# A hybrid pooling and state-space layer on one core: masks, far tiles and column constants in another order, and two pieces of the last output in halves

## The chip, the core and the metric

The kernel runs on one core of a Trainium2 chip. The core has a matrix engine (TensorE, PE in the profile, with PEld for its weight loads), VectorE (DVE), ScalarE (ACT), GpSimd (POOL), and SyncE (SP), which here only issues DMAs. Sixteen DMA engines move data between HBM and the on-chip memory SBUF. PSUM is the memory into which TensorE accumulates. Each engine works through its own instructions in the order of the program and waits at semaphores for the others.

The metric is the time of one execution in microseconds; several executions are timed, and the median is compared. One further execution is profiled.

## The reference

One step of a layer, for a new stream of 256 frames and for a running stream of 32 more (288 tokens in all, all fp32):

```python
xn = rmsnorm(x, norm_mix_pre)
proj = xn @ w_in            # u | z | xBC | dt
y_pool = pool_mixer(u)      # trailing means over 2/4/8/16 frames, then w_pool
y_ssd, h_last = ssd_mixer(z, xbc, dt)   # causal conv, exact chunked scan, SiLU gate, grouped norm
mix = concatenate([y_pool, y_ssd]) @ w_out
x = x + rmsnorm(mix, norm_mix_post)
hn = rmsnorm(x, norm_ffn_pre)
f = (silu(conv(hn @ w_up)[gate]) * conv(hn @ w_up)[value]) @ w_down
x = x + rmsnorm(f, norm_ffn_post)
...
y = (y_diag + y_off).reshape(b, s, G, J, P) + D[..., None] * xh   # in the scan: D is ssd_d, one per head
h_last = decay * h0 + states
```

Outputs are x for both streams and the new states: the pooling rows, the rows of both convolutions, and `h_last`.

## The kernel before

**Layout.** Activations lie with channels on the 128 partitions and the 288 tokens along the row, one tile for each 128 channels. The input has `KD` = 16 tiles, the scan 16 tiles of two heads each (`xs`), the FFN 88 up tiles and 44 input tiles of w_down.

**Products in fp32r.** Each fp32 operand is split into a rounded high part and the rest. ACT copies the high part (`whi`, line 152), VectorE subtracts (`wlo`, line 153), and TensorE makes three products (high by high, high by low, low by high; `mm3`, line 166). `project` does this for groups of 128 output columns: weights come from HBM in pieces (`raw`, four buffers, sent by SP, line 137), are split into `whi` and `wlo` (four buffers each), and are multiplied, in k groups such as (0, 8), (8, 8). The first project of the FFN takes k in four groups of four tiles, and four weight pieces for each group (three of two column tiles and one of one).

**What sets the order.** The framework orders instructions by a timeline of its own, except where `pin` (keep_in_program_order) fixes them among each other, and where `issue_after` puts one behind another. A DMA waits for its buffer, and SP's DMAs go out in order.

**The stages,** in order of time:

1. The start (to 47 us). The pieces `w_first` of the first 768 columns come in 11 chunks (`CHUNKS`), are split by `prepare` (lines 318 to 344) and multiplied (line 397). Beside that the squares of the input are summed for the first norm: `squares` has ACT square two tiles at a time and VectorE add them to a sum (lines 351 to 354), through one buffer, after the chunks that `SQUARES` names. Two `prs` products (line 391) add over partitions, and `rstd` is made of them (lines 394 and 395).
2. The mixer (to 290 us). 8 rounds of `xs` projects, then 8 of `z`. A round's conv is `conv_in` and `conv_out`, with a tanh on ACT. For the scan, heads go in 8 quads. `ssd_masks` (lines 645 to 658) makes a quad's decay mask on ACT (12 Relu, one Exp) and VectorE; `XS_RATE` and `Z_RATE` say in which rounds. `run_pair` multiplies the two quads that stand ready (lines 678 to 684), in the rounds of `PAIR_XS` and `PAIR_Z`. The column constants `dcol` (line 583) hold, for each partition, D for the skip connection (16 columns) and the state's last decay (32): TensorE makes them from `pick`, `sel64` and `hv` with two products (lines 575 and 576).
3. The output product w_out (to 464 us), with the new scan state between.
4. The input of the FFN (464 to 515 us). Line 1087 gives `rm`, the factor of the norm. For each of 16 tiles VectorE multiplies by `rm` (line 1119). The residual is added for tiles 0 to 7 (`NEAR`) by VectorE from SBUF (line 1121), for tiles 8 to 15, the far ones, by a DMA of POOL that adds while it writes (line 1123). Then `hn_of` makes the FFN's input: ACT the high part (line 1100) and a square (line 1108), VectorE the low part (line 1101) and the sum of squares (line 1115). The tiles are done in order 0 to 15. Meanwhile TensorE already multiplies with the tiles that are ready (first project of w_up).
5. The FFN (to 1290 us) and the tail. At the end the token-major output y_prompt is written in 8 pieces of 128 tokens by 512 columns (256 KB each): four for tokens 128 to 255, then four for tokens 0 to 127, together the last 1 MB. For these last four, `rf` is the norm's factor. Piece 0 is made by TensorE (identity times the residual, plus a diagonal matrix of `rf` times the FFN's result, lines 1385 and 1389), copied by ACT (line 1390) and sent by ACT (line 1393). Pieces 1 to 3 are made by VectorE and sent by SP (`y_out`, lines 1367 and 1368).

Of the kernel before, what the change touches and what calls it, by code (L numbers as in the profile page):

```python
# [1 line left out]

# [6 lines left out]
F32 = mybir.dt.float32  # L9
# [3 lines left out]
AX = mybir.AxisListType  # L13
# [26 lines left out]
XS_RATE = (0, 0, 1, 0, 1, 0, 0, 1)  # L40
# [11 lines left out]
    ("f_b", 2 * NF), ("hist_f", 2 * 2 * NF),  # L52
# [4 lines left out]
NEAR = 8  # L57
W_GAP = 48
# [11 lines left out]
def body(  # L70
# [190 lines left out]
    hp = side1.tile([HEADS, 3], F32, name="hp")  # L261
# [26 lines left out]
    id32 = ident[:HEADS, :HEADS]  # L288
# [67 lines left out]
    SQUARES = {4: (0,), 5: (1,), 6: (2,), 7: (3, 4), 8: (5,), 9: (6,), 10: (7,)}  # L356
# [3 lines left out]
    for i, (kb, n) in enumerate(CHUNKS):  # L360
# [26 lines left out]
        for q, (r, m, k, x) in enumerate(products):  # L387
            if i == len(CHUNKS) - 2 and q == 24:
                p_ = aux([P, NT], "prs")
                for c in (slice(0, NT), slice(NT, 2 * NT)):  # L390
                    pin(pe.matmul(p_, ones_r, sq_r[:, c], start=c.start == 0, stop=c.start > 0))
# [5 lines left out]
            pin(pe.matmul(  # L397
                first[m], w[r][:, k, m * P : (m + 1) * P], xn[kb + k][:, x, :],
                start=kb + k + r + x == 0, stop=kb + k == KD - 1 and r == 1,
            ))  # L400
# [13 lines left out]
    act.activation(g_ssd, col["ssd_norm"], AF.Copy, scale=0.5)  # L414
    start.close()
# [4 lines left out]
    sel = mp.tile([HEADS, 2], F32, name="sel")  # L420
    pick = mp.tile([HEADS, NX], F32, name="pick")
    sel64 = mp.tile([HEADS, 2, 64], F32, name="sel64")
    with tc.issue_after(last_split[1].ins):
        dve.tensor_reduce(sel, id32.rearrange("h (t r) -> h r t", r=2), axis=AX.X, op=ALU.add)
        dve.tensor_reduce(pick, id32.rearrange("h (t r) -> h t r", r=2), axis=AX.X, op=ALU.add)
        dve.tensor_copy(sel64, sel.unsqueeze(2).broadcast_to([HEADS, 2, 64]))
# [19 lines left out]

    def conv_out(i, e, out):
# [11 lines left out]
        act.activation(th, c, AF.Tanh)  # L459
# [104 lines left out]
    p_t = aux([P, 10 * HEADS + NX], "ptok")  # L564
    p_tok = p_t[:, : 9 * HEADS].rearrange("p (b h) -> p b h", b=3)
# [3 lines left out]
    hv = htile("hv", NX + HEADS)  # L569
# [5 lines left out]
    follow(pe.matmul(p_[:, :NX], sel64.rearrange("h r q -> h (r q)"), hv[:, :NX], start=True, stop=True))  # L575
    follow(pe.matmul(p_[:, NX:], ones[:HEADS, :], hv[:, NX:], start=True, stop=True))
# [5 lines left out]
    dcol = const.tile([P, NX + HEADS], F32, name="dcol")  # L582
    dve.tensor_copy(dcol, p_)
# [48 lines left out]
    def ssd_masks(q):  # L632
# [55 lines left out]
    def ssd_add(q, ys):  # L688

        for i in range(2):  # L690
            t = 2 * q + i
            for c, y in zip((slice(0, NP_), slice(NP_, NT)), ys[i]):
                o = xs[t][:, c]
                dve.scalar_tensor_tensor(o, o, dcol[:, t : t + 1], y, op0=ALU.mult, op1=ALU.add)
# [266 lines left out]

    bt_h, bt_l = (op_.tile([P, 2, 2, P], F32R, name=n) for n in ("bt_h", "bt_l"))
# [52 lines left out]
    def history(g):  # L1015

        for i in range(2):
# [5 lines left out]
            w = dcol[:, NX:][:, heads]  # L1023
# [94 lines left out]
    for s in range(KD):  # L1118
# [5 lines left out]
        while todo and todo[0] + (1 if todo[0] < NEAR else NEAR) <= s:  # L1124
# [238 lines left out]
    def y_out(q, b, rf):  # L1363
# [3 lines left out]
        pin(dve.scalar_tensor_tensor(x, f_, rf, x, op0=ALU.mult, op1=ALU.add))  # L1367
        pin(sp.dma_start(out=y_prompt[0][b * P : (b + 1) * P, 512 * q : 512 * (q + 1)], in_=x))
# [15 lines left out]
    p_y = acc_ps.tile([P, 512], F32, tag="acc", name="py_")  # L1384
    pin(pe.matmul(p_y, ident, xr[0], start=True, stop=False))
# [3 lines left out]
    pin(pe.matmul(p_y, diag, ft[0], start=False, stop=True))  # L1389
    pin(act.activation(xr[0], p_y, AF.Copy))  # L1390
    y_out(1, 0, rf[:, 0:1])
    y_out(2, 0, rf[:, 0:1])
    pin(act.dma_start(out=y_prompt[0][0:P, 0:512], in_=xr[0]))
# [10 lines left out]
def _laid_out(v, np):  # L1404
# [6 lines left out]
    def groups(a):  # L1411
# [10 lines left out]
        v["state_ffn_conv"],  # L1422
# [7 lines left out]
        "heads": np.stack([v[n][0] for n in ("ssd_dt_bias", "ssd_a_log", "ssd_d")], axis=1),  # L1430
# [32 lines left out]
```

## Time and profile before

| | |
|---|---|
| median of the runs | 1305.62 us (1305.27 to 1305.78, 3 runs) |
| profiled execution, own time | 1306.34 us |
| its span in the profile | 1304.6 us |
| busy, share of the span | PE 99%, PEld 99%, DVE 69%, ACT 51%, POOL 19% |
| granted clock of TensorE | 1.000 |
| mean DMA rate | 193 GB/s, 251.75 MB moved |

The span goes from the first to the last instruction; the own time of the execution is longer, since it takes in what lies before and behind. A row of a timeline gives the start in microseconds, the time, the engine, the line, the operation, the tiles written and read, how many were merged, and in brackets how long the engine was idle before and what ended it. A row of a group gives busy time and mean nanoseconds of one, then idle time before. A row of the waits gives total, times and longest. A row of the chain of waits gives start, duration, engine and line of the chain that ended last. A row of DMA issues gives kilobytes each and the median time from issue to landing.

### The profile page before, as it was taken

What the parts mean: (1) busy time and instruction counts of PE and PEld (TensorE: products, weight loads), DVE (VectorE), ACT (ScalarE), POOL (GpSimd) and SP (SyncE); (2) the same over time, 40 slices, a digit from 0 to 9 for tenths busy, and PEclk for the clock granted to TensorE, in tenths of its full rate; (3) what the DMA queues carried; (4) which work ended last, traced back from release to release, by engine and by line L of the source; (5) the groups of instructions that cost most, each with busy time, mean ns of one, the idle gap of its engine ahead of it and who ended that gap; (6) DMA issues with size and microseconds to landing.
All of it is one profiled execution on the core that took longest, in us unless ns stands there. A gap on an engine that the chain in (4) does not pass through costs nothing.

```text
span 1304.6 us, 25289 instructions
## 1 busy us (share of the span) xinstructions
PE 1296.9 (99%) x10043; PEld 1286.6 (99%) x10043; DVE 897.0 (69%) x1531; ACT 671.6 (51%) x1013; POOL 251.7 (19%) x399
## 2 busy tenths in 40 slices
PE   9999999999999999999999999999999999999998
PEld 9999999999999999999999999999999999999997
DVE  7999987989655588867766744336666666664454
ACT  7557676646544567554544433334444454444442
POOL 2343231222222231211211100001111111201110
PEclk9999999999999999999999999999999999999999
DMA  8668877445767478766545455455545555466663
GB/s 329 204 211 274 250 242 232 137 166 169 242 213 229 140 198 259 210 185 202 172 162 166 160 170 175 157 175 182 174 162 166 175 175 165 163 233 191 209 182 113
DMA packets 110326, 251.75 MB, mean 193 GB/s; under 512 B 64768, under 2 KB 73888, under 8 KB 87936
## 3 DMA queue, kind: packets, MB, share of 16 engines
q1 hardware_dynamic: 103856, 233.36, 55.7%
q0 software_dynamic: 5824, 16.13, 4.3%
q8 instruction: 78, 1.28, 0.4%
q10 hardware_dynamic: 528, 0.66, 0.2%
q14 instruction: 40, 0.33, 0.1%
HBM read 237.11 MB, written 13.00 MB: 192 GB/s over the span
## 4 chain that ended last, share of the span: by engine, by line
PE 96%; DMA 1%; DVE 1%; ACT 1%; issue 0%; SPq 0%; ACTq 0%
PE acc L166 91%; PE acc_x L166 1%; DMA raw<-in_w_first 1%; PE py L678 1%; PE acc L1324 0%; DVE w L334 0%; PE acc L1325 0%; DMA xg<-in_x_g 0%; PE acc_t L1347 0%; DVE sq L354 0%; PE py L680 0%; PE acc_x L397 0%; PE acc L397 0%; DVE xn L321 0%; PE pst L1036 0%
## 5 line engine op out<-in xcount | busy, mean ns | idle before, releaser
L153 DVE TENSOR_TENSOR wlo<-raw,whi 128x1024 fp32r<-128x1024 f32 (+1 forms) x396 | 472.7, 1196 | 297.1 <-ACT whi L152 296.1
L152 ACT ACTIVATE whi<-raw 128x1024 fp32r<-128x1024 f32 (+1 forms) x396 | 408.0, 1033 | 471.1 <-PE acc L166 381.3
L166 PE MATMUL acc<-hn,whi 128*128 128x288 f32 x2752 | 539.0, 294 | 0.5 <-ACT hn L1100 0.4
L166 PEld LDWEIGHTS acc<-hn,whi 128*128 128x128 f32 x2752 | 436.3, 188 | 1.5 <-ACT hn L1100 0.8
L166 PE MATMUL acc<-hn,wlo 128*128 128x288 f32 x1376 | 399.6, 291 | 0.0
L166 PEld LDWEIGHTS acc<-hn,wlo 128*128 128x128 f32 x1376 | 259.0, 188 | 0.0
L166 PE MATMUL acc<-fa,whi 128*128 128x288 f32 x1320 | 257.5, 293 | 0.0
L166 PE MATMUL acc<-xn,whi 128*128 128x288 f32 x1216 | 238.5, 294 | 0.0
L166 PEld LDWEIGHTS acc<-fa,whi 128*128 128x128 f32 x1320 | 208.9, 188 | 0.0
L166 PEld LDWEIGHTS acc<-xn,whi 128*128 128x128 f32 x1216 | 192.9, 188 | 0.6 <-issue 0.5
L166 PE MATMUL acc<-fa,wlo 128*128 128x288 f32 x660 | 192.1, 291 | 0.0
L166 PE MATMUL acc<-xn,wlo 128*128 128x288 f32 x608 | 177.4, 292 | 0.0
L166 PEld LDWEIGHTS acc<-fa,wlo 128*128 128x128 f32 x660 | 124.3, 188 | 0.0
L1150 POOL COPY fc_stage<-ebuf 128x4 f32<-128x4 f32 x88 | 26.9, 306 | 472.8 <-DVE ebuf L1149 451.4
L166 PEld LDWEIGHTS acc<-xn,wlo 128*128 128x128 f32 x608 | 114.5, 188 | 0.0
L166 PE MATMUL acc<-mixs,whi 128*128 128x288 f32 x512 | 100.2, 293 | 0.0
L1145 POOL COPY ebuf<-cols 128x2 f32<-128x2 f32 x88 | 71.7, 816 | 111.1 <-DVE fc L1156 91.8
L1156 DVE SCALAR_TENSOR_TENSOR fc<-ebuf,cols,fc 128x290 f32<-128x290 f32 x176 | 90.5, 518 | 3.5 <-ACT fc L1154 0.8
L1154 ACT ACTIVATE fc<-ebuf,cols 128x290 f32<-128x290 f32 x88 | 54.4, 623 | 72.4 <-DVE ebuf L1149 72.4
L166 PEld LDWEIGHTS acc<-mixs,whi 128*128 128x128 f32 x512 | 81.1, 188 | 0.0
L166 PE MATMUL acc<-mixs,wlo 128*128 128x288 f32 x256 | 74.6, 291 | 0.0
L166 PE MATMUL acc<-mixp,whi 128*128 128x288 f32 x256 | 50.1, 293 | 0.0
(323 smaller groups left out, 1245.3 us busy)
## 6 DMA issues: line engine op xcount, KB each, us to landing
raw<-in_w_up SPq DMA_DIRECT2D x80, 1024.0 KB, 5.1
raw<-in_w_in SPq DMA_DIRECT2D x38, 1024.0 KB, 5.3
raw<-in_w_down SPq DMA_DIRECT2D x32, 1024.0 KB, 5.0
raw<-in_w_out SPq DMA_DIRECT2D x22, 1024.0 KB, 5.2
raw<-in_w_down SPq DMA_DIRECT2D x16, 768.0 KB, 4.4
raw<-in_w_up SPq DMA_DIRECT2D x14, 512.0 KB, 4.6
gb<-g_d POOLq DMA_DIRECT2D x8, 832.0 KB, 6.4
raw<-in_w_first SPq DMA_DIRECT2D x5, 768.0 KB, 13.0
```

Source lines behind the costliest of these rows:

```text
L152: act.activation(hi, raw[:, k : k + n, :], AF.Copy)
L153: dve.tensor_tensor(lo, raw[:, k : k + n, :], hi.bitcast(F32), op=ALU.subtract)
L166: ins = pe.matmul(out, w, a[:, x, :], start=start and n == 0, stop=stop and n == 2)
L678: ins = pe.matmul(y[c, 0:256], xw[:, 0, f_], m[:, h, 0:256], start=True, stop=False)
L1145: pool.tensor_copy(e[:, 258:260], hist_f[:, :, i])
L1150: pool.tensor_copy(fc_stage[:, :, :, i], e[:, 256:324].rearrange("p (s c) -> p s c", c=34)[:, :, 0:2])
L1154: act.activation(c, e[:, 0:290], AF.Identity, bias=col["f_b"][:, i : i + 1], scale=f_w[:, 0, i : i + 1])
L1156: dve.scalar_tensor_tensor(c, e[:, r_ : r_ + 290], f_w[:, r_, i : i + 1], c, op0=ALU.mult, op1=ALU.add)
```

## The change

Several parts, all in one kernel function and its tables:

- `SQUARES`: tiles 2 and 3 are squared behind chunk 4 too, each later pair one chunk earlier, and no chunk has two pairs after that. The two `prs` products stand at the beginning of the last chunk's products instead of at product 24 of the one before.
- `XS_RATE`: quads 0, 1, 2 are masked in xs rounds 5, 6, 7 instead of 2, 4, 7. The first quad's Relu and the Exp of `ce` are put behind a tanh.
- `dcol`, and `sel`, `pick`, `sel64`, `hv` with it, are gone. D comes as 16 more columns of the constants that are loaded at the start (`skip`, repeated over partitions by the host's layout), and the last decay goes out to HBM (`e_d`) and back in to all partitions (`kept`), two small DMAs of SP.
- The turns of the far tiles: after tiles 0 to 3 the order is 8, 4, 9, 5, 10, 6, 11, 7, 12, 13, 14, 15, and `hn_of` of a near tile is called at the turn of the next near one; those of tiles 7 to 15 after all turns.
- The tail: VectorE's first of the last four pieces (piece 1) is made and sent in two halves of 256 columns. Piece 0 has two PSUM tiles of 256 columns; each half is multiplied, copied and sent by itself, the first by SP, the second by ACT.

```diff
-XS_RATE = (0, 0, 1, 0, 1, 0, 0, 1)
+XS_RATE = (0, 0, 0, 0, 0, 1, 1, 1)
...
-    SQUARES = {4: (0,), 5: (1,), 6: (2,), 7: (3, 4), 8: (5,), 9: (6,), 10: (7,)}
+    SQUARES = {4: (0, 1), 5: (2,), 6: (3,), 7: (4,), 8: (5,), 9: (6,), 10: (7,)}
...
-            if i == len(CHUNKS) - 2 and q == 24:
+            if i == len(CHUNKS) - 1 and q == 0:
...
-    dve.tensor_scalar(hv[:, 0:NX], pick, hp[:, 2:3], None, op0=ALU.mult)
-    dve.tensor_scalar(hv[:, NX:], id32, elast, None, op0=ALU.mult)
-    p_ = p_t[:, 9 * HEADS :]
-    follow(pe.matmul(p_[:, :NX], sel64.rearrange("h r q -> h (r q)"), hv[:, :NX], start=True, stop=True))
-    follow(pe.matmul(p_[:, NX:], ones[:HEADS, :], hv[:, NX:], start=True, stop=True))
+    e_d = dram.tile([HEADS, 1], F32, name="e_d")
+    sp.dma_start(out=e_d, in_=elast)
...
-            act.activation(ce, gb[:, :, 384:], AF.Exp)
+        with ExitStack() as order:
+            if not q:
+                order.enter_context(tc.issue_after(tanhs[-1].ins))
+            act.activation(ce, gb[:, :, 384:], AF.Exp)
...
-                    if exps:
-                        order.enter_context(tc.issue_after(exps[-1].ins))
+                    order.enter_context(tc.issue_after((exps or tanhs)[-1].ins))
...
+    kept = const.tile([P, HEADS], F32, name="kept")
+    sp.dma_start(out=kept, in_=e_d.rearrange("h o -> o h").broadcast_to([P, HEADS]))
...
-    for s in range(KD):
+    turns = list(range(FAR_AT))
+    for near, far in zip_longest(range(FAR_AT, NEAR), range(NEAR, KD)):
+        turns.extend(t for t in (far, near) if t is not None)
+    for s in turns:
...
-        while todo and todo[0] + (1 if todo[0] < NEAR else NEAR) <= s:
+        while todo and todo[0] < s < NEAR:
             hn_of(todo.pop(0))
...
-    def y_out(q, b, rf):
+    def y_out(q, b, rf, pieces=1):
...
-        pin(dve.scalar_tensor_tensor(x, f_, rf, x, op0=ALU.mult, op1=ALU.add))
-        pin(sp.dma_start(out=y_prompt[0][b * P : (b + 1) * P, 512 * q : 512 * (q + 1)], in_=x))
+        n = 512 // pieces
+        for c in range(0, 512, n):
+            o = x[:, c : c + n]
+            pin(dve.scalar_tensor_tensor(o, f_[:, c : c + n], rf, o, op0=ALU.mult, op1=ALU.add))
+            pin(sp.dma_start(out=y_prompt[0][b * P : (b + 1) * P, 512 * q + c : 512 * q + c + n], in_=o))
...
-    p_y = acc_ps.tile([P, 512], F32, tag="acc", name="py_")
-    pin(pe.matmul(p_y, ident, xr[0], start=True, stop=False))
+    halves = [(c, acc_ps.tile([P, 2 * P], F32, tag="acc", name="py_")) for c in (slice(0, 2 * P), slice(2 * P, 4 * P))]
+    for c, p_y in halves:
+        pin(pe.matmul(p_y, ident, xr[0][:, c], start=True, stop=False))
...
-    pin(pe.matmul(p_y, diag, ft[0], start=False, stop=True))
-    pin(act.activation(xr[0], p_y, AF.Copy))
-    y_out(1, 0, rf[:, 0:1])
+    y_out(1, 0, rf[:, 0:1], 2)
+    for (c, p_y), by in zip(halves, (sp, act)):
+        pin(pe.matmul(p_y, diag, ft[0][:, c], start=False, stop=True))
+        pin(act.activation(xr[0][:, c], p_y, AF.Copy))
+        pin(by.dma_start(out=y_prompt[0][0:P, c], in_=xr[0][:, c]))
     y_out(2, 0, rf[:, 0:1])
-    pin(act.dma_start(out=y_prompt[0][0:P, 0:512], in_=xr[0]))
```

How this moves instructions is shown at three places.

ACT at the input of the FFN, before: `hn` is the high part of a tile (its input `mg_5227` is far tile 8, `mg_5244` 9, `mg_5452` 10), `sq` its square, and `whi` from `raw_6333` the first weight split of the third k group (k 8 to 11), `raw_6335` and `raw_6337` the second and third.

```order
L1100 ACTIVATE hn_6036<-mg_5050,cols_125 128x288
L1108 ACTIVATE sq_6039<-mg_5050 128x288
L1100 ACTIVATE hn_6056<-mg_5227,cols_125 128x288
L1108 ACTIVATE sq_6059<-mg_5227 128x288
L152 ACTIVATE whi_6341<-raw_6333 128x1024
L1100 ACTIVATE hn_6062<-mg_5244,cols_125 128x288
L152 ACTIVATE whi_6369<-raw_6335 128x1024
L1108 ACTIVATE sq_6065<-mg_5244 128x288
L1100 ACTIVATE hn_6068<-mg_5452,cols_125 128x288
L152 ACTIVATE whi_6397<-raw_6337 128x1024
```

The same place now (the high parts of tiles 7 to 10 stand in a row ahead; `mg_5460` is tile 11, `mg_5819` 12, `mg_5836` 13, `mg_5885` 14; `raw_6324` and `raw_6326` the first and second weight piece of k 8 to 11):

```order
L1094 ACTIVATE hn_6065<-mg_5460,cols_125 128x288
L1102 ACTIVATE sq_6044<-mg_5041 128x288
L1094 ACTIVATE hn_6071<-mg_5819,cols_125 128x288
L1094 ACTIVATE hn_6077<-mg_5836,cols_125 128x288
L1102 ACTIVATE sq_6050<-mg_5218 128x288
L1102 ACTIVATE sq_6056<-mg_5235 128x288
L1102 ACTIVATE sq_6062<-mg_5443 128x288
L1094 ACTIVATE hn_6083<-mg_5885,cols_125 128x288
L153 ACTIVATE whi_6332<-raw_6324 128x1024
L1102 ACTIVATE sq_6068<-mg_5460 128x288
L153 ACTIVATE whi_6360<-raw_6326 128x1024
```

The first split of k 8 to 11 stood behind the high part of tile 8; it now stands behind that of tile 14.

VectorE at the same stage, now: the multiplications by `rm` of the far tiles 8 (`mg_5218`) and 9 (`mg_5235`) between those of the near tiles 4 (`mg_4782`) and 5 (`mg_4799`).

```order
L1116 TENSOR_TENSOR mg_5218<-mg_5218,rm_5933 128x288
L1116 TENSOR_TENSOR mg_4782<-mg_4782,rm_5933 128x288
L1118 TENSOR_TENSOR mg_4782<-mg_4782,xT2_4169 128x288
L1095 SCALAR_TENSOR_TENSOR hn_5997<-mg_4611,cols_125,hn_5997 128x288
L1109 TENSOR_TENSOR msum_4170<-msum_4170,sq_5990 128x288
L1116 TENSOR_TENSOR mg_5235<-mg_5235,rm_5933 128x288
L1116 TENSOR_TENSOR mg_4799<-mg_4799,rm_5933 128x288
```

Before, all but the first of the far multiplications stood in one row behind tile 7's low part; now tiles 8 to 11 each stand ahead of a near tile's, and 12 to 15 together behind two weight splits and tile 6's low part.

ACT in the start, before: `raw_117` and `raw_119` are the weight chunks 7 and 8, `xn` the high parts of the input's tiles, `sq` the squares.

```order
L330 ACTIVATE w_383<-raw_117 128x1536
L353 ACTIVATE sq_392<-xg_95 128x576
L353 ACTIVATE sq_395<-xg_95 128x576
L318 ACTIVATE xn_436<-xg_95 128x288
L318 ACTIVATE xn_437<-xg_95 128x288
L330 ACTIVATE w_435<-raw_119 128x1536
```

and now:

```order
L330 ACTIVATE w_386<-raw_117 128x1536
L353 ACTIVATE sq_395<-xg_95 128x576
L318 ACTIVATE xn_436<-xg_95 128x288
L318 ACTIVATE xn_437<-xg_95 128x288
L330 ACTIVATE w_435<-raw_119 128x1536
```

One square less stands between the chunks 7 and 8; it stands behind chunk 4.

More of the change, by code (lines that the diff above doesn't have):

```diff
@@ L1 @@
 from contextlib import ExitStack
+from itertools import zip_longest
 import concourse.bass as bass
@@ L260, in body @@
     pin(sp.dma_start(out=cols, in_=cols_in))
-    hp = side1.tile([HEADS, 3], F32, name="hp")
+    hp = side1.tile([HEADS, 2], F32, name="hp")
     pin(sp.dma_start(out=hp, in_=heads_in))
@@ L419, in body @@
     mp = mixer.enter_context(tc.tile_pool(name="mixer", bufs=1))
[L420 to L426, printed above, removed]
     sc_stage = const.tile([P, 2, 3, NXC], F32, name="sc_stage")
@@ L693, in ssd_add @@
                 o = xs[t][:, c]
-                dve.scalar_tensor_tensor(o, o, dcol[:, t : t + 1], y, op0=ALU.mult, op1=ALU.add)
+                dve.scalar_tensor_tensor(o, o, skip[:, t : t + 1], y, op0=ALU.mult, op1=ALU.add)
     def token_sums(p_, sq, first_, last_, pin=False):
@@ L1022, in history @@
             o = h.rearrange("p (r q) -> p r q", r=4)
-            w = dcol[:, NX:][:, heads]
+            w = kept[:, heads]
             dve.tensor_tensor(o, o, w.unsqueeze(2).broadcast_to([P, 4, 64]), op=ALU.mult)
@@ L1429, in _laid_out @@
         "cols": np.concatenate([on_partitions(a) for a in cols], axis=1),
[L1430 removed]
+        "heads": np.stack([v[n][0] for n in ("ssd_dt_bias", "ssd_a_log")], axis=1),
         "state_nq": v["state_ssd"].reshape(D_SSD, P).T,
```

18 lines of the change are left out of this document (8 added, 10 removed).

## The prediction, made before the changed kernel had run

> **What bounds the kernel now.** I read the page first, then the waits of TensorE, then its timeline around each wait, and the other engines' timelines at the same places. From the page and from the waits of TensorE's matmuls:
>
> ```profile
> span 1304.6 us, 25289 instructions
> PE 1296.9 (99%) x10043; PEld 1286.6 (99%) x10043; DVE 897.0 (69%) x1531; ACT 671.6 (51%) x1013; POOL 251.7 (19%) x399
> ...
> PE acc L166 <- ACT hn L1100: 0.4, 1, 0.4
> ```
>
> TensorE (PE) is busy for 99% of the span and its waits are single events, the longest behind the start in the tail (shown there). So a microsecond is saved only where TensorE computes less, where one of its few waits goes, or behind its last product. Any other saving on VectorE (DVE), ScalarE (ACT) or a queue is covered by TensorE, and any new order on them costs nothing until a product finds its weight or its input missing. I go through the change by the places where TensorE does less or could wait.
>
> **The start.** Timelines of ACT, DVE and PE, on the first eleven weight pieces:
>
> ```profile
> 25.65 0.68 ACT L353 ACTIVATE sq<-xg 128x576 f32<-128x576 f32 x1 [1.93 <-DVE sq L354]
> ...
> 27.09 1.47 ACT L330 ACTIVATE w<-raw 128x1536 fp32r<-128x1536 f32 x1
> ...
> 18.42 1.76 DVE L334 TENSOR_TENSOR w<-raw,w 128x1536 fp32r<-128x1536 f32 x1 [0.31 <-ACT w L330]
> ...
> 28.60 1.76 DVE L334 TENSOR_TENSOR w<-raw,w 128x1536 fp32r<-128x1536 f32 x1
> ...
> 38.32 0.46 DVE L379 TENSOR_TENSOR sq_r<-sq,sq_r 128x288 fp32r<-128x288 f32 x1
> ...
> 20.36 3.30 PE L397 MATMUL acc<-xn,w 128*128 128x288 f32 x24
> ...
> 29.74 0.42 PE L397 MATMUL acc<-xn,w 128*128 128x288 f32 x2
> 30.41 3.20 PE L397 MATMUL acc<-xn,w 128*128 128x288 f32 x22 [0.25 <-DVE w L334]
> ...
> 38.34 0.89 PE L391 MATMUL prs<-sq_r,ones_r 128*128 128x288 f32 x2
> 39.07 1.74 PE L397 MATMUL acc_x<-xn,w 128*128 128x288 f32 x12
> ```
>
> Two squares stand together behind weight piece 7. They share one buffer, so the second waits 1.93 us on ACT for VectorE's add, and the split of piece 8 behind it starts only at 27.09 on ACT and ends on VectorE at 30.36 (28.60 + 1.76). A steady product takes 0.131 us (the 12 of the row at 39.07: 1.74 less the 0.16 by which the last one's end trails its start slot). After the two at 29.74 the next was due at 30.00 and came at 30.41: 0.41 lost. The two `prs` products should take 0.26 and the next row starts 0.73 after them, since the second half of `sq_r` ended only at 38.78: 0.47 lost. The change puts one square behind each piece and the second extra one at piece 4, so ACT is up to 1.9 us earlier at piece 8, VectorE some 1.4 us earlier from there on, and both losses go; `prs` is also moved behind 12 products more, 1.6 us of additional cover. What is late next: the square added at piece 4 delays the split of piece 6 by about 0.6 us (ACT 0.68), so VectorE's part ends near 20.8 rather than 20.18, and TensorE wants it for the third product of the row at 20.36, at 20.62. I charge 0.1. The later `rstd` frees the PSUM banks 1.2 us later at most, which the next project, at 47.5 us, does not see. **Start: -0.8** (bounds: -0.9 with nothing late at piece 6, 0 if the load of a piece decides instead).
>
> **The column constants.** TensorE no longer makes `dcol`. From the chain of waits:
>
> ```profile
> 106.45 0.32 PE ptok L575 x2
> 106.77 0.24 PE ptok L576 x2
> ```
>
> These products are on the path and go: **-0.55** (bounds -0.56 and -0.4, as their neighbours may take over part of a pipeline fill). In place of them come two tiny DMAs on SP's queue. The second waits for the first to land, and weight loads stand behind it; the nearest row is
>
> ```profile
> g_d<-g SPq DMA_DIRECT2D x1, 52.0 KB, 1.6
> ```
>
> so one load could start 1.6 us late. TensorE's lead covers that (next part); uncovered it would be 1.6 us once. VectorE loses seven small instructions; it does not set the path.
>
> **The mixer's masks.** Quads 0 and 1 move from xs rounds 2 and 4 to rounds 5 and 6. Waits of ACT and groups of VectorE between 110 and 150 us and between 85 and 150 us:
>
> ```profile
> ACT whi L152 <- PE acc L166: 13.0, 8, 2.0
> ...
> L658 DVE TENSOR_TENSOR m<-m,cbt 128x1664 f32<-128x1664 f32 x2 | 3.8, 1889 | 0.0
> ...
> L645 DVE TENSOR_TENSOR xk<-xk,tok 128x768 f32<-128x768 f32 x3 | 2.9, 955 | 0.0
> ```
>
> ACT waits for TensorE to free weight buffers, so the splits run ahead of the products by their four buffers. A mask costs VectorE 1.89 + 0.96, the same work as before in other rounds. I charge 0. If the lead is used up in the three rounds in a row, TensorE waits for about one mask, 2.9 us.
>
> **The normalised input of the FFN.** This is the term that decides. Rows of DVE, POOL, ACT and PE, the landing time of the far tiles, and VectorE's split of a weight piece:
>
> ```profile
> 471.32 0.45 DVE L1119 TENSOR_TENSOR mg<-mg,rm 128x288 f32<-128x288 f32 x1
> ...
> 472.98 0.45 DVE L1119 TENSOR_TENSOR mg<-mg,rm 128x288 f32<-128x288 f32 x1
> ...
> 483.66 2.67 DVE L1119 TENSOR_TENSOR mg<-mg,rm 128x288 f32<-128x288 f32 x7
> ...
> 480.37 0.85 POOL L1123 DMA_DIRECT2D mg<-in_x_g  x1 [9.32 <-DVE mg L1119]
> 484.40 6.18 POOL L1123 DMA_DIRECT2D mg<-in_x_g  x7 [3.19 <-DVE mg L1119]
> ...
> 486.17 0.54 ACT L1100 ACTIVATE hn<-mg,cols 128x288 fp32r<-128x288 f32 x1 [4.95 <-DMA mg<-in_x_g]
> ...
> 487.11 1.06 ACT L152 ACTIVATE whi<-raw 128x1024 fp32r<-128x1024 f32 x1
> 489.85 0.54 ACT L1100 ACTIVATE hn<-mg,cols 128x288 fp32r<-128x288 f32 x1 [1.68 <-DMA mg<-in_x_g]
> ...
> 490.26 0.70 PE L166 MATMUL acc<-hn,whi 128*128 128x288 f32 x4
> ...
> 492.54 1.11 PE L166 MATMUL acc<-hn,whi 128*128 128x288 f32 x4
> ...
> mg<-in_x_g POOLq DMA_DIRECT2D x8, 144.0 KB, 6.0
> ...
> L153 DVE TENSOR_TENSOR wlo<-raw,whi 128x1024 fp32r<-128x1024 f32 (+1 forms) x396 | 472.7, 1196 | 297.1 <-ACT whi L152 296.1
> ```
>
> Now: far tile 8 is sent at 480.37 and lands 5.8 us later, tile 9 at 484.40 and 5.45 later; ACT waits for both. But the first weight split of the third k group (k 8 to 11) stands ahead of tile 9 in ACT's order, is done at 488.17, and TensorE takes it at 490.26. What TensorE loses is in the two rows of four products: 1.11 against 0.70, so 0.4.
>
> After the change VectorE sends far tiles between near ones. A near tile takes 1.66 us (471.32 to 472.98), a far multiplication 0.38 (2.67 over 7). Tile 8 is multiplied at 471.3, and 9, 10, 11 each 2.04 later, the last at 477.4. Tile 7, two splits (2 x 1.2) and the rest of a near tile (1.28) follow, so tiles 12 to 15 are multiplied from 477.8 + 0.4 + 2.4 + 1.3 = 481.9. POOL starts 0.3 behind a product (480.37 against 480.07), and each issue takes 0.88 (6.18 over 7): tile 14 starts at 482.6 + 1.76 = 484.4. It lands 5.45 to 6.0 later, 489.8 to 490.4.
>
> All far tiles land earlier than before, so the waits for them shrink. But ACT's new order has hn of tiles 7 to 14 and four squares ahead of the first split of k 8 to 11, which moved from behind tile 8 to behind tile 14. So that split starts at 490.1 + 0.44 and ends at 491.6: TensorE, due at 490.26, starts near 491.65 and loses 1.4. Its next four products (0.52) use that piece, then it needs the second split, which stands behind one square (0.33 + 1.06): ready near 493.0, another 0.8. VectorE's part of the splits, and the squares' sums, queue behind the same waits, but TensorE asks for them later. Sum 2.2, less the 0.4 of now: **+1.8**. Bounds: -0.4 if tile 14 lands before 488.4, so that nothing waits; +3.3 if the tiles ahead of it and the weight loads on the same queues make it 1.5 later, an estimate, as no row shows four such DMAs behind spread ones.
>
> [...]
>
> **The tail.** Rows of ACT, PE, DVE, SP, and landing times:
>
> ```profile
> 1297.41 0.38 ACT L1381 ACTIVATE sq<-acc_t 128x256 f32<-128x256 f32 x1 [2.18 <-PE acc_t L1347]
> ...
> 1298.45 0.40 ACT L1388 ACTIVATE diag<-ident,rf 128x128 f32<-128x128 f32 x1 [0.24 <-DVE rf L1259]
> 1300.07 0.60 ACT L1390 ACTIVATE xr<-py__15355 128x512 f32<-128x512 f32 x1 [1.22 <-PE py__15355 L1389]
> 1300.69 0.36 ACTq L1393 DMA_DIRECT2D out<-xr  x1
> ...
> 1298.90 1.12 PE L1389 MATMUL py__15355<-ft,diag 128*128 128x512 f32 x2 [0.67 <-ACT diag L1388]
> ...
> 1298.45 1.42 DVE L1367 SCALAR_TENSOR_TENSOR xr<-ft,rf,xr 128x512 f32<-128x512 f32 x2
> ...
> 1297.35 3.54 SPq L1368 DMA_DIRECT2D out<-xr  x4
> ...
> out<-xr SPq DMA_DIRECT2D x7, 256.0 KB, 2.2
> ...
> out<-xr ACTq DMA_DIRECT2D x1, 256.0 KB, 2.6
> ```
>
> The last landing is ACT's: 1300.69 + 2.6 = 1303.3; SP's last is issued at about 1300.55 and lands at 1302.8. In halves TensorE's first product ends at 1299.47, ACT copies 256 columns in 0.38 (the square of as many, from PSUM too) by 1299.9, SP sends it; the second product ends at 1300.04, its copy at 1300.43, and ACT sends 128 KB at 1300.45, landing in some 2.4: 1302.85. On SP the piece of ACT stands ahead of VectorE's last two, and SP has two issues more (0.33 each), so its last goes near 1300.65 and lands at 1302.85. VectorE pays one more start, 0.08. **Tail: -0.4** (bounds -0.5, and +0.1 where SP's last decides).
>
> **Sum:** -0.8 - 0.55 + 0 + 1.8 - 0.4 = +0.05 us on the span of 1304.6. The profiled execution took 1306.34 by its own time, 0.72 above the median 1305.62 of the runs; the difference is carried over, so 1306.4 there and a median of **1305.7**. The terms' bounds put this case within 1304.2 to 1307.3.
>
> **Rivals.** (a) The far tiles land sooner, because eight spread DMAs no longer queue behind one another: then the new wait and the old one are both gone, +1.8 becomes -0.4, and the time is 1305.7 - 2.2 = 1303.5. For it: four of them are sent 2 us apart rather than 0.88; against it: tile 8 was alone on its queue and still took 5.8. (b) Slower: in xs rounds 5 to 7 three masks in a row use up VectorE's lead, and TensorE waits for a `wlo` in one of them, from the point where VectorE falls over 2 us behind its present place (the longest wait of ACT for TensorE above). Price one mask, 2.9: 1308.6. For it: the third mask falls into the round that also adds the pair's products; against it: rounds 2 and 4 get lighter by as much, and ACT waits for TensorE there. (c) The halves bring nothing, as SP's last piece, behind ACT's, ends the run 0.1 later: -0.4 becomes +0.1, 1306.2.
>
> **Chances.** Forecast 0.55, (a) 0.20, (b) 0.17, (c) 0.08. A measurement of this kernel tells some 0.2%, 2.6 us, from no change: below 1303.0 is faster, above 1308.2 slower. Half of (a) and a little of the forecast's low side lie below: 0.15. Most of (b) and a little more lie above: 0.20. The rest, 0.65, is no change. The range runs from inside (a) to (b): 1302.8 to 1308.8.
>
> **What would show it.** Start: no wait of TensorE at piece 8, `prs` two products in 0.26. Constants: no product between `ptok`'s transposes and `pcb`. FFN input: ACT waiting for a far tile, and TensorE for `whi`, about 22 us behind the first `hn` product, over 1.5 us in all; no such wait means (a). Mixer: a wait of TensorE before 290 us means (b). Tail: the last landing 0.4 nearer to the end of `diag`. The forecast is wrong if the span moves by more than 2 us.

## The result, and the profile after

| | before | after |
|---|---|---|
| median of 7 runs | 1305.27 us (1304.76 to 1305.78) | 1309.65 us (1307.59 to 1311.11) |
| ratio | | 1.0034, 95% interval 1.0023 to 1.0044 |
| profiled execution, own time | 1306.34 us | 1311.11 us |
| its span | 1304.6 us | 1309.4 us |

The change makes the kernel slower by 0.34%, 4.4 us. The forecast was 1305.7 us, with a range up to 1308.8. The profiled execution of the changed kernel is the slowest of its seven, so its single terms add up to 4.8 us and not to 4.4.

From the page and the waits of TensorE, after:

```profile
span 1309.4 us, 25285 instructions
PE 1298.0 (99%) x10043; PEld 1288.8 (98%) x10043; DVE 898.2 (69%) x1526; ACT 671.9 (51%) x1014; POOL 256.7 (20%) x399
...
PE acc L167 <- ACT whi L153: 3.1, 2, 2.6
...
PE py__15346 L1392 <- ACT diag L1389: 1.2, 1, 1.2
```

As many matmuls as before, 1.1 us more of their busy time, and one new wait that stands above all others: two waits of products (`acc`) for a weight split (`whi`), 3.1 us in all. It is the wait that the prediction spoke of, and larger.

The input of the FFN, after: timeline of POOL, then ACT, then PE:

```profile
482.06 3.52 POOL L1120 DMA_DIRECT2D mg<-in_x_g  x4 [3.31 <-DVE mg L1116]
...
488.10 1.19 ACT L1094 ACTIVATE hn<-mg,cols 128x288 fp32r<-128x288 f32 x2 [4.89 <-DMA mg<-in_x_g]
...
491.25 0.54 ACT L1094 ACTIVATE hn<-mg,cols 128x288 fp32r<-128x288 f32 x1 [0.66 <-DMA mg<-in_x_g]
491.69 1.04 ACT L153 ACTIVATE whi<-raw 128x1024 fp32r<-128x1024 f32 x1
492.63 0.43 ACT L1102 ACTIVATE sq<-mg 128x288 f32<-128x288 f32 x1
492.96 1.04 ACT L153 ACTIVATE whi<-raw 128x1024 fp32r<-128x1024 f32 x1
...
489.89 0.29 PE L167 MATMUL acc_x<-hn,wlo 128*128 128x288 f32 x1
492.78 0.79 PE L167 MATMUL acc<-hn,whi 128*128 128x288 f32 x4 [2.59 <-ACT whi L153]
494.06 1.13 PE L167 MATMUL acc<-hn,whi 128*128 128x288 f32 x4 [0.49 <-ACT whi L153]
494.99 0.44 PE L167 MATMUL acc<-hn,wlo 128*128 128x288 f32 x1
495.23 0.68 PE L167 MATMUL acc<-hn,whi 128*128 128x288 f32 x2
```

Read it upwards. TensorE was due at 490.03 (489.89 and one product) and started at 492.78, when the first split of k 8 to 11 was done. That split stood behind the high part of tile 14, which ACT could make only when the tile had landed, at 491.25. And behind the wait the products no longer follow in 0.131 us: from 494.99 to 495.23 is 0.24. Two windows of TensorE show why (busy time and count of matmuls, then the granted clock, DMA share and GB/s):

```profile
490.90:494.31 3.41, 1.04 (x6) 1.00 0.08 19
494.31:497.72 3.41, 3.41 (x16) 0.50 0.66 178
```

For 3.41 us (494.31 to 497.72) TensorE had half of its clock. (Windows that reach over the edges of this stretch average it with full clock, and so give 0.57 or 0.58.) Elsewhere in this stage it has 1.00.

A second loss has no wait at all. One window of the mixer's first products, before, then after:

```profile
60.00:100.00 40.00, 40.00 (x310) 1.00 0.69 206
```

```profile
60.00:100.00 40.00, 40.00 (x302) 1.00 0.65 196
```

TensorE is busy throughout at full clock in both, and makes 8 products fewer in 40 us: from start to start 133.3 ns for each instead of 130.0.

The table follows the same products through the profiles of all kernels: how much sooner (minus) or later (us) each starts than in the profile of before, where it starts at the time in the head. Differences between neighbouring columns are what a stage cost. The executions differ by themselves too, above all in the start: five profiles with the old start lie 1.5 us apart in the first column.

| kernel | first product of the mixer, 47.50 | first `py`, 150.45 | first `hn` product, 467.78 | first of w_down, 744.71 | first of the tail's `py_`, 1297.21 | end, 1304.60 |
|---|---|---|---|---|---|---|
| changed kernel | -0.89 | -0.23 | -0.26 | +4.22 | +4.19 | +4.79 |
| turns undone | -1.65 | -0.99 | -1.03 | -1.08 | -1.11 | -1.06 |
| only turns | -1.27 | -1.27 | -1.28 | +1.37 | +1.37 | +1.37 |
| only tail | -1.17 | -1.17 | -1.17 | -1.57 | -1.57 | -1.34 |
| only start | -0.82 | +0.59 | +2.34 | +2.50 | +2.50 | +2.50 |
| changed, order kept | -1.45 | -2.19 | -2.22 | +0.79 | +0.77 | +1.16 |
| changed, split first | -1.80 | -1.15 | -1.18 | -1.05 | -1.07 | -1.03 |
| changed, wait filled | -0.87 | -0.20 | -0.24 | +2.94 | +2.92 | +3.38 |
| changed, far tiles spread | -1.50 | -0.85 | -0.88 | +2.31 | +2.29 | +2.87 |
| start, constants, masks, order kept | -1.29 | -2.03 | -2.06 | -2.44 | -2.47 | -2.53 |
| only start, order kept | -1.10 | -0.54 | +0.37 | -0.16 | -0.16 | -0.17 |
| only masks | -0.41 | -0.40 | -0.40 | +0.02 | +0.02 | +0.02 |
| only constants | +0.27 | +3.74 | +3.71 | +2.96 | +2.94 | +2.87 |

For the changed kernel: start -0.89, then +0.66 up to `py`, +4.48 at the input of the FFN, +0.60 in the tail.

### The profile page after: what moved, and what is told of

It reads as the page before. It is cut to its first block, busy times and chain, and to the rows that moved or that the text cites. A ratio compares the mean times of both kernels' runs of the same rounds, so it can differ in the third digit from the quotient of the medians.

```text
span 1309.4 us, 25285 instructions
## 1 busy us (share of the span) xinstructions
PE 1298.0 (99%) x10043; PEld 1288.8 (98%) x10043; DVE 898.2 (69%) x1526; ACT 671.9 (51%) x1014; POOL 256.7 (20%) x399
## 3 DMA queue, kind: packets, MB, share of 16 engines
q8 instruction: 78, 1.28, 0.4%
## 4 chain that ended last, share of the span: by engine, by line
PE 95%; DMA 2%; issue 1%; ACT 1%; DVE 1%; POOL 0%; ACTq 0%; SPq 0%; DVEq 0%; POOLq 0%
PE acc L167 90%; PE acc L397 1%; DMA raw<-in_w_first 1%; PE acc_x L167 1%; DMA mg<-in_x_g 1%; PE py L670 1%; PE acc_x L397 1%; PE acc L1321 0%; PE acc L1322 0%; POOL mg L1120 0%; PE py L672 0%; DMA raw<-in_w_up 0%; DVE xr L1367 0%; PE acc_t L1344 0%; ACT w L330 0%
## 5 line engine op out<-in xcount | busy, mean ns | idle before, releaser
L1142 POOL COPY ebuf<-cols 128x2 f32<-128x2 f32 x88 | 74.6, 848 | 117.0 <-DVE fc L1153 93.3
```

Of the source, the lines that this page charges most:

```text
L1142: pool.tensor_copy(e[:, 258:260], hist_f[:, :, i])
```

## The experiments

Each time is the median of 6 to 11 runs, beside 24 to 33 runs of the kernel before on the same chip. Three groups of four ran together; the kernel before had 1305.14, 1305.05 and 1305.76 us in them.

**The turns undone.** All of the change, but the far tiles in their old places.

```diff
-    turns = list(range(FAR_AT))
-    for near, far in zip_longest(range(FAR_AT, NEAR), range(NEAR, KD)):
-        turns.extend(t for t in (far, near) if t is not None)
-    for s in turns:
+    for s in range(KD):
...
-        while todo and todo[0] < s < NEAR:
+        while todo and todo[0] + (1 if todo[0] < NEAR else NEAR) <= s:
```

> All of the change but the new turns of the far tiles, which go 0 to 15 again. Theory (the first split of k 8 to 11 behind the high part of far tile 14, and the slow products behind that wait, cost about 4.4 us): the wait of 2.75 us is gone, products at 493 to 498 us take 0.131 us, and the time falls from 1309.65 to about 1305.2 (1304.4 to 1306.0). Rival (the loss lies in the slower products between 50 and 100 us and in the tail, 1.2 and 0.6 us, and the wait only shows what is lost anyway): over 1307.

Measured: 1305.43 us, ratio 1.0002 (0.9993 to 1.0011). The wait for `whi` is not among TensorE's waits any more, and the loss of 4.4 us is gone with it. What is left of the change is worth nothing, where the prediction had -1.75 for it.

**Only the turns,** in the kernel before (the edit above the other way round).

> The kernel before with nothing but the new turns of the far tiles. Theory: the whole wait and the slow products are there, about 4.4 us on the time of before, 1309.7 (1308.5 to 1310.5), the first product of the third k group near 492.8. Rival (the wait needs the other parts, as these put TensorE or the loads elsewhere in time): under 1307.5.

Measured: 1309.12 us, ratio 1.0029 (1.0020 to 1.0038). The turns alone cost 4.0 us. From the timelines of ACT and PE of this kernel:

```profile
486.51 0.54 ACT L1102 ACTIVATE hn<-mg,cols 128x288 fp32r<-128x288 f32 x1 [4.32 <-DMA mg<-in_x_g]
...
490.15 1.04 ACT L154 ACTIVATE whi<-raw 128x1024 fp32r<-128x1024 f32 x1
...
491.25 0.80 PE L168 MATMUL acc<-hn,whi 128*128 128x288 f32 x4 [2.12 <-ACT whi L154]
492.53 0.80 PE L168 MATMUL acc<-hn,whi 128*128 128x288 f32 x4 [0.48 <-ACT whi L154]
```

The same chain, 1.5 us earlier than in the changed kernel (491.25 against 492.78), since TensorE came to this stage 1.0 us sooner (-1.28 against -0.26 in the table) and the tiles landed sooner. The granted clock stays at 1.00 behind this wait, and the stage costs 2.65 us (-1.28 to +1.37). This execution, 1307.67 us, is the fastest of the ten: the others are up to 3.3 us longer.

**Only the tail,** in the kernel before.

```diff
-    p_y = acc_ps.tile([P, 512], F32, tag="acc", name="py_")
+    halves = [(c, acc_ps.tile([P, 2 * P], F32, tag="acc", name="py_")) for c in (slice(0, 2 * P), slice(2 * P, 4 * P))]
...
-    y_out(1, 0, rf[:, 0:1])
+    y_out(1, 0, rf[:, 0:1], 2)
```

> The kernel before with nothing but the halves in the tail. Theory, by the trace of the changed kernel (the last piece of SP goes 2.50 us behind the start of diag instead of 2.1, as it stands behind ACT's first half): +0.3 us, 1305.6; the 0.54 us by which ACT's square came late there is not part of it. Rival 1 (as predicted): -0.4, 1304.9. Rival 2 (the late square belongs to the halves too, since two more products stand in front of it or ACT's issue is longer): +0.9, 1306.2.

Measured: 1305.78 us, ratio 1.0003 (0.9994 to 1.0012). The runs can't tell it from no change; the table has +0.23 from the tail's `py_` to the end. No gain of the halves is to be seen.

**Only the start,** in the kernel before.

```diff
-    SQUARES = {4: (0,), 5: (1,), 6: (2,), 7: (3, 4), 8: (5,), 9: (6,), 10: (7,)}
+    SQUARES = {4: (0, 1), 5: (2,), 6: (3,), 7: (4,), 8: (5,), 9: (6,), 10: (7,)}
...
-            if i == len(CHUNKS) - 2 and q == 24:
+            if i == len(CHUNKS) - 1 and q == 0:
```

> The kernel before with the new places of the squares and of the two prs products only. Theory: the first product of the mixer comes 0.9 us sooner, and the products between 50 and 100 us keep 130.0 ns: 1304.4. Rival (the earlier start of the mixer's first project, not another part, brings the 133.3 ns products): the 0.9 us is lost again by 107 us, 1305.6.

Measured: 1307.70 us, ratio 1.0022 (1.0012 to 1.0033): slower than either theory had it. Its window from 60 to 100 us has 302 products, so the slower rate came with this part. And two waits in the mixer came as well. From the timelines of DVE and PE:

```profile
166.29 0.48 DVE L212 STREAM_TRANSPOSE blocks<-xs 128x288 f32<-128x288 f32 x1 [2.90 <-DMA xs_d<-blocks]
...
170.16 1.88 DVE L658 TENSOR_TENSOR m<-m,cbt 128x1664 f32<-128x1664 f32 x1
171.96 0.95 DVE L645 TENSOR_TENSOR xk<-xk,tok 128x768 f32<-128x768 f32 x1
...
174.06 2.35 DVE L153 TENSOR_TENSOR wlo<-raw,whi 128x1024 fp32r<-128x1024 f32 x2
...
175.33 0.40 PE L166 MATMUL acc<-xn,wlo 128*128 128x288 f32 x1 [0.73 <-DVE wlo L153]
```

VectorE waits 2.90 us for a transfer, then has a mask (1.88 and 0.95) ahead of the low part of a weight, and TensorE waits for that.

**The order of the products kept.** What made the rate? TensorE waits for nothing there, but the order of its products differs. With H and L for the high and low part of the weights, h and l for those of the input, the first weight piece of the mixer's first project has eight groups of three, one for each k and column tile. Before, and after:

```
before   HhLhHl HhLhHl HhLhHl HhLhHl HhLhHl HhLhHl HhLhHl HhLhHl
after    HhLhHl HhLhHl HhLhHl HhLhHl HhHlHh LhHlHh LhHlHh LhHlHh LhHlLh
```

In the program both read `Hh Lh Hl` there and `Hh Hl Lh` in all later pieces (two letters a product). The ninth group of the second line already reaches into the next piece. These products are not pinned, and the framework pulled the second half of the first piece apart in the changed program. One entry in a table pins them:

```diff
-WHOLE = (20, 21)
+WHOLE = (20, 21, 1)
```

> The changed kernel, with the three products of each weight column of the mixer's first project kept together in the order that they are written in (high by high, low by high, high by low in the first piece); in the changed kernel the framework had pulled them apart. Theory (the order in that first piece decides at which of two steady rates the next 465 products run): the products between 50 and 107 us fall from 133.3 to 130.0 ns, and the time by 1.2 to 1.5 us, 1308.3. Rival (the rate comes from where the start ends in time, or from the data layout): 133.3 ns stay, 1309.6.

Measured: 1308.70 us, ratio 1.0027 (1.0018 to 1.0036). The window from 60 to 100 us, then:

```profile
60.00:100.00 40.00, 40.00 (x310) 40.00 (x309) 39.77 (x97) 21.45 (x31) 14.39 (x16) 1.00 0.66 194
```

310 products again. In the two traces eight places in the order of TensorE's products differ, all among the first 25, and nothing in the order of ACT, VectorE and POOL. From the mixer's first product to `py` this kernel takes 1.40 us less than the changed one (-0.74 against +0.66). The runs show 0.7 of it (4.38 us above before against 3.65): the wait at the FFN became longer as TensorE came sooner, 2.67 us idle ahead of it in this profile.

**The split first.** The high parts of tiles 12 to 15 (`todo` of 12 and up) are made by a function that the FFN's first project calls, and stand behind the second split of k 8 to 11 on ACT. Their squares got three buffers of their own. The heart of the edit:

```diff
+        with tc.issue_after(splits[1].ins):
+            while todo:
+                hn_of(todo.pop(0))
```

> The changed kernel with its new turns, but the high parts of the far tiles 12 to 15 put behind the first two weight splits of k 8 to 11, in the program and in ACT's order. Theory (the loss is the split queued behind the high part of tile 14, nothing else of the turns): the wait at 490 us goes, and with it the old one at tile 9, so 4.2 us less than the changed kernel and 0.4 less than with the turns undone: 1305.1 (1304.3 to 1305.9). Rival (the loads of the weight pieces themselves are late, since the far tiles are sent beside them): a wait of over 1.5 us stays there, 1307.5 or more.

Measured: 1306.03 us, ratio 1.0005 (0.9996 to 1.0014). TensorE's wait, from the waits of this kernel:

```profile
PE acc L169 <- ACT whi L155: 0.4, 1, 0.4
```

The stage costs +0.13 in the table, with the new turns in it, and the time is 1.0 us over the kernel before, where the changed kernel has 4.4. So it is the place of the split that cost most of it, not the order in which the far tiles are multiplied and sent. But with the turns undone the stage has -0.05: even so the turns gain nothing.

**The wait filled.**

```diff
+            if (kb, n) == (8, 4):
+                fill = aux([P, NT], "fill")
+                for _ in range(20):
+                    pin(pe.matmul(fill, acts[7][:, 0, :P], acts[7][:, 0, :], start=True, stop=True))
```

> The changed kernel with 20 products more (2.6 us, their result is not used) in TensorE's order ahead of the third k group, where it waits 2.75 us. Theory (behind a wait of that length TensorE gets a lower clock for some 4 us, which the profile of the changed kernel shows as 0.57 to 0.58): no lower clock behind the filled wait, 1.5 us less where it happened, so a median near 1308.3 and a narrower spread than the 3.5 us of the changed kernel. Rival (the 240 ns products come from contention at the weights, or the lower clock has another cause): same products of 240 ns, 1309.6 or, if the filling reaches past the wait, more.

Measured: 1308.91 us, ratio 1.0027 (1.0017 to 1.0038), its seven runs from 1308.25 to 1309.68. From the timeline of PE:

```profile
490.02 2.80 PE L189 MATMUL fill<-hn 128*128 128x288 f32 x20
493.23 0.80 PE L167 MATMUL acc<-hn,whi 128*128 128x288 f32 x4 [0.41 <-ACT whi L153]
494.51 0.80 PE L167 MATMUL acc<-hn,whi 128*128 128x288 f32 x4 [0.48 <-ACT whi L153]
```

No product of 0.24 us behind it, although the piece came as late as before, and the stage costs 1.3 us less than in the profile of the changed kernel (3.18 against 4.48). The median is 0.7 us below the changed kernel's, where the theory had 1.35, and the seven runs lie within 1.4 us instead of 3.5.

**The far tiles spread.**

```diff
+    turns = [t for near in range(NEAR) for t in (near, near + NEAR)]
```

> The changed kernel with one far tile behind each near one from the first: 0, 8, 1, 9, ... 7, 15, so that tile 14 is sent near 480.5 us and not in a row of four. Theory (the four sent together near 482 to 485.6 us, with two weight pieces beside them, take 6.0 to 8.6 us; those sent one at a time take 3.3 to 4.7): tile 14 lands before 486, ACT waits less, TensorE's wait at 490 falls under 0.5 us, 1305.5 to 1306. Rival (the landing is set by the weight pieces that share the queues): tile 14 lands after 488, 1307.5 or more.

Measured: 1309.54 us, ratio 1.0034 (1.0022 to 1.0046). My expectation was wrong, and ACT's timeline shows why:

```profile
481.12 3.53 ACT L1094 ACTIVATE hn<-mg,cols 128x288 fp32r<-128x288 f32 x8
...
488.86 0.54 ACT L1094 ACTIVATE hn<-mg,cols 128x288 fp32r<-128x288 f32 x1 [3.88 <-DMA mg<-in_x_g]
...
491.40 1.99 ACT L153 ACTIVATE whi<-raw 128x1024 fp32r<-128x1024 f32 x2
```

Tiles 7 to 14 are all there by 484.65 without a wait, as expected. But the framework now put the split behind tile 15, and four squares behind it. The wait moved to the last tile. The expectation went by when tile 14 lands, and not by what the split would then stand behind.

**The best of it:** the changed kernel with the turns and the tail undone, and the order of the products kept.

> The changed kernel without the new turns of the far tiles and without the halves in the tail, and with the three products of each weight column of the mixer's first project kept in their written order. Theory (start -0.5, constants -0.6, masks 0 are gains once the first project's products run at 130.0 ns): 1.5 us less than with only the turns undone, and 0.1 to 0.3 less for the old tail, so some 1303.6 (1303.0 to 1304.3) where the kernel before has 1305.1. Rival (the 1.5 us are given back at a later wait, as TensorE comes sooner to the mixer's masks or to the far tiles): 1305.0.

Measured: 1304.43 us (1303.42 to 1304.93), ratio 0.9989 (0.9980 to 0.9998). It is faster than both kernels, by 1.3 us than the one before, where 1.5 was expected.

**Only the start, with the order kept.**

> The kernel before with the new start alone, and the products of the mixer's first project kept in their written order: four rows of TensorE's order differ from the run with the new start alone, none on another engine. Theory (the order of these products sets the rate up to 107 us): 130.0 ns there, 1.5 us less than that run's 1307.7, so 1306.2, with the two waits for the low parts of weights at 168 and 175 us still there or longer. Rival (the rate follows from where the start ends): 133.3 ns, 1307.7.

Measured: 1306.80 us, ratio 1.0008 (0.9999 to 1.0017): 1.0 us over the kernel before, where the start alone was 2.6 over it, so the order is worth 1.5 us in the runs, as expected. The products take 130.0 ns up to 107 us (309 of them from 60 to 100 us). One of the two waits in the mixer is still there, 0.5 us.

From the first product to `py` it loses 0.56 us where the start alone lost 1.41. These 0.56 us come from the slower rate as well, at another place. A row of PEld, then two windows of PE:

```profile
133.98 0.19 PEld L166 LDWEIGHTS acc<-xn,wlo 128*128 128x128 f32 x1 [0.15 <-DVE wlo L153]
...
120.00:132.00 12.00, 12.00 (x95) 1.00 0.85 273
136.00:148.00 12.00, 12.00 (x92) 1.00 0.94 286
```

A weight load waits 0.15 us for VectorE, and behind it the products run at 133.3 ns up to `py`, in the same order as ahead of it. Before, both windows have 94.

**Only the masks.**

> The kernel before with nothing but the masks of quads 0 to 2 in rounds 5, 6, 7 and their order behind a tanh. Theory (the masks cost nothing by themselves; they matter only with the new start, which without them waits in rounds of the mixer): 1305.1, no wait of TensorE between 110 and 290 us. Rival, as in the prediction (three masks in a row use up VectorE's lead): a wait of some 2.9 us there, 1308.

Measured: 1305.62 us, ratio 0.9999 (0.9990 to 1.0008), no wait in the mixer. The rival of three masks in a row falls.

**Only the constants.**

> The kernel before with nothing but D as a loaded column and the last decay through HBM. Theory: the two products behind the transposes are gone, 0.55 to 0.65 us, the products up to 107 us stay at 130.0 ns: 1304.6. Rival (the two small DMAs on SP's queue make the weight loads behind them late, or the new order on VectorE brings a wait): 1305.3 or more.

Measured: 1308.22 us, ratio 1.0018 (1.0009 to 1.0027). The two products are gone, but the mixer loses more. From the timelines of ACT and PE:

```profile
113.81 0.31 ACT L605 ACTIVATE ce<-gb 128x128 f32<-128x128 f32 x1 [8.08 <-DMA gb<-g_d]
...
121.25 0.40 PE L167 MATMUL acc<-xn,wlo 128*128 128x288 f32 x1 [1.45 <-DVE wlo L154]
```

ACT stands 8.08 us at the first Exp of `ce`, waiting for a transfer, with weight splits behind it. This is the instruction that the change puts behind a tanh, and the masks that follow are those that it moves.

## Why the prediction failed, point by point

**FFN input, +1.8: mis-sized, and the step that failed.** The mechanism was as described: hn of tile 14, the split behind it, TensorE waiting for `whi` near 490, then for the second split. It cost 4.48 us in the profile, and in the runs 4.0 (only the turns) to 4.2 (1309.65 against 1305.43 with them undone). The step "It lands 5.45 to 6.0 later, 489.8 to 490.4" was wrong. The tile was third of four in a row of issues, and landed 8.1 us behind its issue, so that ACT could take it at 491.25. The prediction took the first landing of a row and the median of the group for one near its end, and the profile of before had the rest of it in one line. That line of the far tiles' DMAs, before, and the same for tiles 13 and 14 alone, after (8.1 is tile 14's):

```profile
DMA to landing us min/median/max: 5.4/6.0/8.9
```

```profile
DMA to landing us min/median/max: 6.1/7.1/8.1
```

There was luck in it too: the issues of a row start 0.54 us apart and not 0.88, since they overlap (POOL's four take 0.85 to 1.91 us each and 3.52 together), so tile 14 was sent at 483.14 and not at 484.4. Sent at 484.4 and with the same 8.1 us, it would by my estimate from these two numbers have landed another 1.3 us later. Why the last of such a row take longest the runs don't show.

So the first wait is 2.75 us (492.78 less 490.03) and not 1.4. The second is 0.65 and not 0.8. The clock is the part that no step had, put at nothing: 15 products at 0.240 instead of 0.131, 1.6 us. With the 0.4 of before taken off, the sum is 4.6, where the table has 4.48 and the prediction 1.8: 1.2 of the difference are the two waits, 1.6 the clock.

**Start, -0.8: right at its place, lost behind it.** The waits at piece 8 and in `prs` are gone, and the first product of the mixer is 0.89 sooner. Over all profiles, the nine with the new start lie 0.75 us ahead of the five with the old one in the mean; as these five differ by 1.5 us among themselves, the size is not settled. Piece 6 cost 0.35 us (its wait ends at 20.91) where 0.1 was charged. But that the next project "does not see" the new start, as the prediction says of the later `rstd`, was wrong: the order of its products changed, and 1.40 us were lost up to 107 us at a slower steady rate (133.3 ns a product instead of 130.0), a term that the sum had at nothing. What in the new start moved the framework to that order the runs don't show. The prediction goes through the places where something could wait, not through a stretch where nothing does.

**Constants, -0.55:** -0.65 between `ptok` and `pcb` in the profile of the changed kernel. Right, though by themselves they bring a loss in the mixer that I did not see.

**Masks, 0:** right as a sum and wrong as a reading. By themselves they do nothing. But without them VectorE and ACT come to masks and transfers at a wrong time: TensorE loses 1.75 us between `py` and `hn` with the start alone, and 3.47 up to `py` with the constants alone. With start, constants and masks together none of this is left (-0.03 from `py` to `hn`). No run has the masks beside only one of the two, so it is likely but not shown that it is the masks that take the loss away. Rival (b) had the sign turned round.

**Tail, -0.4:** +0.60 in the profile of the changed kernel. Rival (c) was right in kind: the halves gain nothing, as SP's last piece goes later. Rows of ACT and SP, after:

```profile
1303.18 0.40 ACT L1389 ACTIVATE diag<-ident,rf 128x128 f32<-128x128 f32 x1 [0.23 <-DVE rf L1256]
1304.37 0.38 ACT L1393 ACTIVATE xr<-py__15346 128x256 f32<-128x256 f32 x1 [0.79 <-PE py__15346 L1392]
...
1304.78 0.33 SPq L1394 DMA_DIRECT2D out<-xr  x1
1305.20 0.88 SPq L1368 DMA_DIRECT2D out<-xr  x2
```

SP sends ACT's first half 1.60 us behind the start of `diag`, and its last piece ends being issued at 2.90 us (1306.08). Before, that was 2.44 (SP's row ended at 1300.89, `diag` started at 1298.45). The prediction counted 0.33 for each issue; the last two take 0.88. The end comes 6.21 us behind the start of `diag` (1309.38 less 1303.18), where it was 6.15 (1304.60 less 1298.45), and 6.38 with the tail alone: the halves cost 0.05 to 0.23 us.

The other 0.54 of the +0.60 stand ahead of `diag` and are ACT's: an issue took 1.04 us, where it took 0.45 before. From the chain of waits:

```profile
1301.05 1.04 ACTq L1374
1302.10 0.05 issue
1302.14 0.48 ACT sq L1381 x2
```

It stood in front of the last square. This long issue (0.84 to 1.04) is in four kernels of the study and missing in three others with the same tail. The four are those in which the first split of k 8 to 11 comes late; the cause stays open.

**What the forecast's sum had right** was that the FFN's input decides. The bound of +3.3 there, "1.5 later" for the tile, held for the landing (491.22 in the trace) and not for the clock behind it, and the gains set against it were given back by the rate and the tail. The upper bounds of the five terms add up to +3.0, so to 1308.6, and not to the 1307.3 that the prediction gives; 1309.65 lies outside either.

## What to carry to other kernels

When a helper's calls are moved, look at what the framework then queues behind the last of them: here a weight split that TensorE needed next, behind the seventh of eight transfers. For a transfer in a row take the last landing of such a row, not the median (8.9 us against 6.0 before). And compare the order of the matmuls even where nothing waits, and pin it where it was chosen: here another order came with 133.3 ns for each product instead of 130.0.

## What the runs showed of the hardware

**Two steady rates.** The mixer's first project has 449 products in a row on the chain of waits: 58.63 us in the profile of before (from 47.56), 60.03 in that of the changed kernel (from 46.68). Between 60 and 100 us, with no wait and the clock at 1.00, that is 130.0 ns for each product in the one and 133.3 in the other. In each of two pairs of kernels the order of the compute engines differs at eight of TensorE's first 25 products and nowhere else: they have 302 products in those 40 us against 310 (the changed kernel, and with the order kept) and 302 against 309 (only the start, and with the order kept). Of the other profiles, turns undone has 302 there, and only the constants and the best of it 310. Split first, wait filled and far tiles spread take 0.65 to 0.67 us more than before from the mixer's first product to `py`, where the changed kernel takes 0.66 more; only turns, only tail and only masks take 0.00 to 0.01 more. The order is not the only thing that the slower rate came with: in the start with the order kept, a weight load waited 0.15 us at 133.98 us, and 95 products in 12 us ahead of it became 92 behind it. Why there are two rates the runs don't show.

**A wait with half of the clock behind it.** In the profile of the changed kernel 2.59 us of idle time were followed by 3.41 us at a clock of 0.50, with products at 0.240 us, and the clock was 1.00 again from 497.72. Behind the waits of three other profiles it stayed at 1.00: 2.67 us (order kept), 2.12 (only turns) and 1.7 (far tiles spread). In the changed kernel TensorE was idle for 2.37 of the 3.41 us ahead of the fall (the windows above: busy 1.04 of 3.41). With the order kept, two neighbouring windows of that length share the wait of 2.67 us, idle for 1.60 and 1.55:

```profile
486.38:489.79 3.41, 1.81 (x14) 1.00 0.83 177
489.79:493.21 3.42, 1.87 (x12) 1.00 0.05 10
493.21:496.62 3.41, 3.41 (x27) 1.00 0.77 219
```

What decides whether the clock falls behind such a wait was not shown. Over the unfilled kernels (the changed one, only turns, order kept, far tiles spread) 24 of 34 executions had a mean granted clock of 0.997 or 0.998, and in each of these kernels they were in the mean 1.4 to 2.0 us longer than the others; with the wait filled, none of seven had it, nor any of eleven with the turns undone. (One execution each of only the start and only the constants had 0.998 as well.)
